# Attention's score and value products as three fp32r products of high and low parts

## The chip, the cores and the metric

The kernel runs on one core of a Trainium2 chip. The metric is the device time of one execution in microseconds. A profiled execution is read beside it; its times come from the hardware profiler.

## The reference

One block of a hybrid layer on x of 256 rows and 2048 columns, all float32. Cut to what matters here:

```python
hn = rms_norm(x, norm_w)
proj = hn @ w_in          # q, k, v, z_a, z_s, xbc, dt_raw, g_a, g_s
for window, dilation in ((128, 1), (512, 4), (2048, 16)):
    scores = q @ k.T * 128 ** -0.5 + alibi      # per head, 16 heads of 128
    o, lse = softmax(masked scores) @ v, logsumexp(masked scores)
o_a = (sum over patterns of softmax(lse) * o) * silu(z_a)
y = rms_norm(ssd_scan(silu(conv(xbc)), softplus(dt_raw), ...) * silu(z_s), ssm_norm_w)
merged = sigmoid(g_a) * (o_a @ w_attn_branch) + sigmoid(g_s) * (y @ w_ssm_branch)
out = rms_norm(x + merged @ w_out, final_norm_w)
```

With 256 rows the three attention patterns see the same scores under three masks. The kernel computes one softmax over the scores, weighted by how many patterns admit each pair (`count_c`).

## The kernel before

**Products in parts.** Nearly all weights are read once, from `wall`, in units of 128 x 1024 float32 (512 KB). `unit(n)` makes of each a high part `h` (a copy to the type fp32r, ScalarE, L271) and a low part `l` (the difference, VectorE, L272). The activations are kept in the same two parts; a product is then the sum of three fp32r products: high with high, high with low, low with high. `triple` in `gemm_pair` writes them (L471 to L473). `split` (L279, L281) makes the two parts of an activation: a copy on ScalarE, a difference on VectorE. `h` and `l` have four buffers each, `w` five.

**The stages, in order.** The scan's projections (`xs`, `zs`, `B`, `C`, with the scan between), its branch product (`ssm`), `v`, the 16 heads of attention with `q`, `k` and `za` of each head, then `ga`, `attn` and `out`. `ssm`, `v`, `ga`, `attn` and `out` go through `gemm_pair`: blocks of two times 512 columns, in which some groups of four units (`S_QUADS`) take seven products in place of eight. Their extra parts `ht` and `lt` come from the pool `mul`, two buffers each.

**A projection in attention.** `gemm_a` takes two units; each holds eight blocks of 128 x 128 weights, and each block gives one matmul of 512 columns (L324: high weights with both parts of x) and one of 256 (L327: low weights with x's high part): 32 matmuls for each of `q`, `k`, `za`. `evac` adds the two halves of the result: ScalarE copies one out of PSUM (`lo_k`, L378), VectorE adds the other (L380).

**The heads.** `qT` and `kT` are float32, 128 x 256. `scores` (L1022, L1023) multiplies them by float32 matmuls: 128 rows of queries with 128 keys, and the other 128 with all 256. The scores are then scaled, masked and made into `p` (128 x 384) by VectorE and ScalarE (`t`, `st`, `p`). `turn_p` turns the three blocks of `p` on TensorE (L1046, `ptp`) and ScalarE copies them out as `pT` (L1047). `mix` (L1053, L1054) multiplies `vt` and `pT` by float32 matmuls of 256 and of 128 columns, and gates and splits the result into `oaT`. The work is put into the stream of projections by ticks: each projection is a tick, and `after(n, f)` runs f n ticks later. So while head h+1's `q` begins, TensorE has the mix of head h-2, the turn of head h-1 and the scores of head h. A scheduler then sets each engine's order from its own estimates; each engine runs its instructions in that order, and waits where an operand is late.

**Other transfers around it.** `sum_jobs` fetches weights into `th_a` in attention, forms sums on VectorE and stores them for the later stages. `keep_left` stores left factors for the `attn` stage through `sxt_o` (pool `mul`, tag `ht`) to `sxd_o`. In the out stage four blocks of x go to `fin`, each behind a unit of weights: POOL writes one column of the block after that unit's `h` is made (L624), and then SP issues the load (L625). `fin` takes the memory of `vt`.

Of the kernel before, what the change touches and what calls it, by code (L numbers as in the profile page):

```python
# [9 lines left out]
F32 = mybir.dt.float32  # L10
F32R = mybir.dt.float32r
AF = mybir.ActivationFunctionType
# [3 lines left out]
P = 128  # L16
S = 256
# [45 lines left out]
LEFT_EVERY, ATT_EVERY = 11, 4  # L63
SUM_LAG = 3
ROOM_SSM = 2

OFF_Q, OFF_K, OFF_V, OFF_ZA = 0, D, 2 * D, 3 * D
OFF_ZS = 4 * D
# [123 lines left out]
def hybrid_block(ctx: ExitStack, tc: tile.TileContext, wall, xt, x, pk_d, cst_d, fw_d, out):  # L192
# [98 lines left out]
    def two_kts(t, q):  # L291
        t, q = (t[q // 4], q % 4) if isinstance(t, list) else (t, q)
        return t[:, 2 * q : 2 * q + 2, :]
# [4 lines left out]
    def after(ticks, f, inside=0):  # L298

        due.append((now[0] + ticks + inside / 2, f))  # L300
# [53 lines left out]
    def project(tag, acc=None):  # L354
        return gemm_a(tag, lambda kt: XT[:, kt, :], acc)
# [56 lines left out]
    def keep_left(key, x, spare, t):  # L412

        sx = t.bitcast(F32R).rearrange("p (e n s) -> p e n s", e=2, n=4)[:, :, spare:]
        turn_x(sx, t.rearrange("p (n m) -> p n m", n=2), x, spare)
        spill(lefts, key, f"sxd_{key[0]}{key[1]}", sx.bitcast(F32), [2, 4 - spare, P])
# [36 lines left out]

    seats = {}

    def gemm_pair(tag, x_of, n_kt, sxs, swap, extra={}, close=1, order=None, room={}):


# [7 lines left out]

        def banks(ts, s):
            return [bank(t, 4 if t == "g" else 2, f"{s}_{name}_{n}") for n, t in enumerate(ts)]

        def triple(acc, xh, xl, h, l, start, stop):  # L470
            pe.matmul(acc, xh, h, start=start, stop=False)  # L471
            pe.matmul(acc, xh, l, start=False, stop=False)  # L472
            pe.matmul(acc, xl, h, start=False, stop=stop)  # L473

        es = banks(e_tags, "ps")
        prods = []
# [538 lines left out]
    with tc.tile_pool(name="att", bufs=2) as ap:  # L1015
        ev = ap

        oaT = [half_kts("oaTa", "yo0a")]

        def scores(h, q, k, p):  # L1020
            sps = bank("m1", 2, f"sps{h}")
            pe.matmul(sps[:, :P], q[:, :P], k[:, :P], start=True, stop=True)  # L1022
            pe.matmul(sps[:, P:384], q[:, P:], k, start=True, stop=True)  # L1023
            t = cpool.tile([P, 384], F32, name=f"t{h}", tag="ssq")
            slope = 2.0 ** (-8.0 * (h + 1) / NH)
            ve.scalar_tensor_tensor(t, dist_c, slope / SCALE, sps[:, :384], ALU.mult, ALU.add)
            st = ap.tile([P, 8], F32, name=f"st{h}", tag="st", bufs=1)
            parts = ((0, P), (P, 384))
            for i, (a, b) in enumerate(parts):
                ve.tensor_reduce(st[:, i : i + 1], t[:, a:b], mybir.AxisListType.X, ALU.max)  # L1030
            ve.tensor_scalar(st[:, 2:4], st[:, 0:2], -SCALE, None, ALU.mult)
            for i, (a, b) in enumerate(parts):
                ac.activation(p[:, a:b], t[:, a:b], AF.Exp, scale=SCALE, bias=st[:, 2 + i : 3 + i])
            for i, (a, b) in enumerate(parts):
                ve.scalar_tensor_tensor(
                    p[:, a:b], p[:, a:b], 1.0, count_c[:, a:b], ALU.mult, ALU.mult,
                    accum_out=st[:, 4 + i : 5 + i],
                )
            ve.reciprocal(st[:, 6:8], st[:, 4:6])
            for i, (a, b) in enumerate(parts):  # L1040
                ve.tensor_scalar(p[:, a:b], p[:, a:b], st[:, 6 + i : 7 + i], None, ALU.mult)

        def turn_p(h, p, pT):
            tps = bank("m1", 2, f"ptp{h}")
            for i in range(3):
                pe.transpose(tps[:, i * P : (i + 1) * P], p[:, i * P : (i + 1) * P], ident)  # L1046
            ac.activation(pT, tps[:, :384], AF.Copy)  # L1047

        def mix(h, pT, za):
            ops = bank("m2", 2, f"ops{h}")  # L1050
            o = za
            hs = slice(h * P, (h + 1) * P)
            pe.matmul(ops[:, :S], vt[:, 0, hs], pT[:, :S], start=True, stop=False)  # L1053
            pe.matmul(ops[:, P:S], vt[:, 1, hs], pT[:, S:384], start=False, stop=True)  # L1054
            ve.tensor_tensor(o, ops[:, :S], za, ALU.mult)
            if h == 8:
                oaT.append(half_kts("oaTb", "yo0b"))
            split(o, kt_of(oaT, h)[:, :S], kt_of(oaT, h)[:, S:])
            q = h // 2
            if h % 2 == 1 and q in ATT_QUADS:  # L1060
                keep_left(("o", q), two_kts(oaT, q), 0, mul.tile([P, UNIT], F32, name=f"sxt_o{q}", tag="ht", bufs=2))

        sum_jobs(
            SUMS_ATT, range(FIRST[("q", 0)] + 7, N_UNITS, ATT_EVERY),
            [
                (th_a[:, i, :UNIT], th_a[:, 1, UNIT + 512 * i : UNIT + 512 * i + 512], th_a[:, 0, UNIT:])
                for i in range(2)
            ],
        )

        for h in range(NH):
            q, k = (ap.tile([P, S], F32, name=f"{n}T{h}", tag=f"{n}T", bufs=2) for n in "qk")

            for n, d in (("q", q), ("k", k)):
                evac(project((n, h)), d, f"{n}{h}")
            p = ap.tile([P, 384], F32, name=f"p{h}", tag="p", bufs=2)
            pT = ap.tile([P, 384], F32, name=f"pT{h}", tag="pT", bufs=1)
            za = ap.tile([P, S], F32, name=f"za{h}", tag="za", bufs=3)
            after(S_LAG + (6, 4, 2)[max(h - 13, 0)], lambda a=(h, pT, za): mix(*a))
            after(S_LAG + (3 if h < 15 else 1), lambda a=(h, p, pT): turn_p(*a))  # L1080
            after(S_LAG + (h == 0), lambda a=(h, q, k, p): scores(*a))
            zh = ev.tile([P, S], F32, name=f"zah{h}", tag="eh", bufs=2)
            evac(project(("za", h)), zh, f"za{h}", scale=0.5)
            half_silu(zh, za, f"za{h}")

        for n, q in enumerate(ATT_QUADS):
            fetch_left(
                sx_of_o, xl if n else xk, max(1, n and len(SX_X) - 1), ("o", q), two_kts(oaT, q), 0, FIRST[("ga", 2)] + O_BEHIND[n]
            )
        room = {"wt": [th_a[:, i, UNIT:] for i in range(2)]}  # L1090
        for c in (0, 2):
            es, prods = gemm_pair(
                ("ga", c), lambda kt: XT[:, kt, :], KT, sx_of_x, c == 2, order=G_ORDERS[c], room=room
            )
            open_gate(c, es, prods)
        tick(final=True)

    with tc.tile_pool(name="fin", bufs=2) as fp:
# [36 lines left out]
        for n in range(4):  # L1135
            i, cs = n // 2, slice(n % 2 * UNIT, (n % 2 + 1) * UNIT)
            behind_unit(
                FIRST[("out", 0)] + (1, 3, 5, 8)[n],
                lambda behind, i=i, cs=cs: fetch(fin[:, i, cs], x[i * P : (i + 1) * P, cs], behind),
            )  # L1140

# [79 lines left out]
```

## Time and profile before

| | us |
|---|---|
| median of 3 runs | 1387.36 (1385.95 to 1387.86) |
| the profiled execution | 1384.94 |
| its span, first to last instruction | 1383.1 |
| TensorE busy (PE) | 1373.2 |
| weight loads busy (PEld) | 1169.1 |
| VectorE busy (DVE) | 1164.5 |
| ScalarE busy (ACT) | 834.2 |
| GpSimd busy (POOL) | 138.6 |

The granted TensorE clock is 0.999 of full speed. In the rows below, a line gives the engine, the line of the kernel, the operation, the tile written and those read, the shape, and how often. A float32 matmul leaves two records, an fp32r matmul one. Matmuls overlap their ends, so the distance between the starts of two matmuls tells more than the duration of one.

### The profile page before, as it was taken

Reading aid. Unit: us, or ns where it says so; the run is one execution under the profiler, and the core shown is the slowest. Engines: PE = TensorE matmul, PEld = TensorE weight load, DVE = VectorE, ACT = ScalarE, POOL = GpSimd, SP = SyncE. Lnnn points to the kernel's source line nnn. Section 1 sums busy time; section 2 is a strip of 40 time slices with the busy share of each in tenths; the row PEclk is TensorE's granted clock in tenths of the full one; section 3 lists DMA queues with packets and bytes.
Section 4 is the critical chain, followed back from the end, with each engine's and each line's share of the span. In section 5 each row is a group of like instructions: output and inputs, shape, how many; then the busy total and the mean of one; then the engine's idle time right before and its main releaser. Section 6 shows DMA issues by size and latency. Waiting matters only on the chain.

```text
span 1383.1 us, 20652 instructions
## 1 busy us (share of the span) xinstructions
PE 1373.2 (99%) x7260; PEld 1169.1 (85%) x7260; DVE 1164.5 (84%) x1742; ACT 834.2 (60%) x1300; POOL 138.6 (10%) x222
## 2 busy tenths in 40 slices
PE   9999999999999999999999999999999999999997
PEld 8888888888888888888888888888888888888886
DVE  7898999987798898788888897777877788888997
ACT  7656677675667675766564554544544556655564
POOL 2301111101011100010000001111111000000110
PEclk9999999999999999999999999999999999999999
DMA  9657888768787866568678558888888747865763
GB/s 342 237 192 228 306 264 281 279 216 279 246 272 232 296 218 204 186 227 279 226 264 287 200 193 279 282 271 280 292 290 299 244 163 263 291 223 180 274 258 107
DMA packets 104648, 343.96 MB, mean 249 GB/s; under 512 B 11680, under 2 KB 13664, under 8 KB 104416
## 3 DMA queue, kind: packets, MB, share of 16 engines
q1 hardware_dynamic: 103824, 341.46, 72.2%
q8 instruction: 57, 0.93, 0.3%
q10 hardware_dynamic: 720, 1.18, 0.2%
q14 instruction: 47, 0.39, 0.1%
HBM read 314.34 MB, written 28.25 MB: 248 GB/s over the span
## 4 chain that ended last, share of the span: by engine, by line
PE 98%; DMA 0%; DVE 0%; POOL 0%; SPq 0%; ACT 0%; issue 0%; POOLq 0%; DVEq 0%; ACTq 0%
PE ps_zs L324 8%; PE ps_xs L324 8%; PE ps_zs L327 4%; PE ps_k L324 4%; PE ps_q L324 4%; PE ps_za L324 4%; PE ps_xs L327 4%; PE ps_ssm L471 3%; PE ps_ssm L472 3%; PE ps_ssm L473 3%; PE ps_q L327 2%; PE ps_k L327 2%; PE ps_za L327 2%; PE ps_gs L409 2%; PE ps_gs L407 2%; PE ps_gs L408 2%
## 5 line engine op out<-in xcount | busy, mean ns | idle before, releaser
L271 ACT ACTIVATE h<-w 128x1024 fp32r<-128x1024 f32 (+1 forms) x400 | 416.0, 1048 | 330.9 <-issue 79.6
L272 DVE TENSOR_TENSOR l<-w,h 128x1024 fp32r<-128x1024 f32 (+1 forms) x400 | 482.1, 1212 | 128.8 <-ACT h L271 126.5
L324 PE MATMUL ps_zs<-XT,h 128*128 128x512 f32 x496 | 176.2, 396 | 0.0
L324 PE MATMUL ps_xs<-XT,h 128*128 128x512 f32 x496 | 175.9, 396 | 0.0
L327 PE MATMUL ps_zs<-XT,l 128*128 128x256 f32 x496 | 139.7, 282 | 0.0
L327 PE MATMUL ps_xs<-XT,l 128*128 128x256 f32 x496 | 139.6, 281 | 0.0
L324 PEld LDWEIGHTS ps_xs<-XT,h 128*128 128x128 f32 x496 | 93.1, 188 | 21.8
L324 PEld LDWEIGHTS ps_zs<-XT,h 128*128 128x128 f32 x496 | 93.1, 188 | 21.4
L327 PEld LDWEIGHTS ps_zs<-XT,l 128*128 128x128 f32 x496 | 93.6, 189 | 1.5 <-issue 0.9
L327 PEld LDWEIGHTS ps_xs<-XT,l 128*128 128x128 f32 x496 | 93.6, 189 | 0.4
L324 PE MATMUL ps_q<-XT,h 128*128 128x512 f32 x256 | 92.3, 404 | 0.0
L324 PE MATMUL ps_k<-XT,h 128*128 128x512 f32 x256 | 89.8, 394 | 0.0
L324 PE MATMUL ps_za<-XT,h 128*128 128x512 f32 x256 | 89.5, 394 | 0.0
L327 PE MATMUL ps_q<-XT,l 128*128 128x256 f32 x256 | 71.0, 277 | 0.0
L327 PE MATMUL ps_k<-XT,l 128*128 128x256 f32 x256 | 71.0, 277 | 0.0
L327 PE MATMUL ps_za<-XT,l 128*128 128x256 f32 x256 | 70.9, 277 | 0.0
L529 ACT ACTIVATE ha<-wa 128x1024 fp32r<-128x1024 f32 x42 | 44.3, 1055 | 35.7 <-PE ps_ssm L473 9.1
L530 DVE TENSOR_TENSOR ltu<-wa,htu 128x1024 fp32r<-128x1024 f32 x42 | 51.3, 1223 | 12.7 <-ACT htu L529 12.5
L530 DVE TENSOR_TENSOR la<-wa,ha 128x1024 fp32r<-128x1024 f32 x42 | 51.3, 1222 | 10.8 <-ACT ha L529 10.6
L529 ACT ACTIVATE htu<-wa 128x1024 fp32r<-128x1024 f32 x42 | 44.3, 1054 | 24.2 <-PE ps_ssm L473 7.2
L324 PEld LDWEIGHTS ps_k<-XT,h 128*128 128x128 f32 x256 | 48.0, 188 | 11.2
L324 PEld LDWEIGHTS ps_za<-XT,h 128*128 128x128 f32 x256 | 48.0, 188 | 11.1
(657 smaller groups left out, 3305.1 us busy)
## 6 DMA issues: line engine op xcount, KB each, us to landing
w<-in_wall SPq DMA_DIRECT2D x396, 512.0 KB, 4.6
wa<-in_wall SPq DMA_DIRECT2D x42, 512.0 KB, 4.9
th_a<-in_wall SPq DMA_DIRECT2D x19, 512.0 KB, 5.4
sums_at<-in_wall SPq DMA_DIRECT2D x18, 512.0 KB, 4.0
acb<-acum_d SPq DMA_DIRECT2D x32, 256.0 KB, 3.7
t_ssm<-sums_at SPq DMA_DIRECT2D x13, 512.0 KB, 4.1
wt<-t_ssm SPq DMA_DIRECT2D x13, 512.0 KB, 5.1
th_a<-in_wall SPq DMA_DIRECT2D x19, 256.0 KB, 5.8
```

The costliest lines, as they stand in the source:

```text
L271: ac.activation(h[:, a:b], w[:, a:b], AF.Copy)
L272: ve.tensor_tensor(l[:, a:b], w[:, a:b], h[:, a:b].bitcast(F32), ALU.subtract)
L324: pe.matmul(acc, h[:, kk, :], m, start=(kt == 0), stop=False)
L327: pe.matmul(acc[:, S:], l[:, kk, :], m[:, :S], start=False, stop=(kt == KT - 1))
L407: pe.matmul(accs[i], xh, h[:, kk], start=(kt == 0), stop=False)
L408: pe.matmul(accs[i], xh, l[:, kk], start=False, stop=False)
L409: pe.matmul(accs[i], xl, h[:, kk], start=False, stop=(kt == KT - 1))
L471: pe.matmul(acc, xh, h, start=start, stop=False)
L472: pe.matmul(acc, xh, l, start=False, stop=False)
L473: pe.matmul(acc, xl, h, start=False, stop=stop)
L529: ac.activation(h, src, AF.Copy)
L530: ve.tensor_tensor(l, src, h.bitcast(F32), ALU.subtract)
```

## The change

Queries and keys are split into high and low parts after `evac` (tiles `qk_parts`, in the two `lt` buffers of the pool `mul`); `qT` and `kT` share one buffer. The turned `p` is split into `pT` and `pl`, and the head's columns of `vt` into `vhl`. The scores and the products with v go through `triple`, which moves out of `gemm_pair`: three fp32r matmuls for each float32 one. The last `sxt_o` takes a part of `th_a` in place of an `ht` buffer. The loads of x for the output go behind the units 1, 5, 9 and 12 of the out stage in place of 1, 3, 5 and 8.

```diff
--- before.py
+++ after.py
@@ -63,6 +63,7 @@
 LEFT_EVERY, ATT_EVERY = 11, 4
 SUM_LAG = 3
 ROOM_SSM = 2
+X_BEHIND = 1, 5, 9, 12
 
 OFF_Q, OFF_K, OFF_V, OFF_ZA = 0, D, 2 * D, 3 * D
 OFF_ZS = 4 * D
@@ -453,6 +454,11 @@
 
     seats = {}
 
+    def triple(acc, xh, xl, h, l, start, stop):
+        pe.matmul(acc, xh, h, start=start, stop=False)
+        pe.matmul(acc, xh, l, start=False, stop=False)
+        pe.matmul(acc, xl, h, start=False, stop=stop)
+
     def gemm_pair(tag, x_of, n_kt, sxs, swap, extra={}, close=1, order=None, room={}):
 
 
@@ -466,11 +472,6 @@
 
         def banks(ts, s):
             return [bank(t, 4 if t == "g" else 2, f"{s}_{name}_{n}") for n, t in enumerate(ts)]
-
-        def triple(acc, xh, xl, h, l, start, stop):
-            pe.matmul(acc, xh, h, start=start, stop=False)
-            pe.matmul(acc, xh, l, start=False, stop=False)
-            pe.matmul(acc, xl, h, start=False, stop=stop)
 
         es = banks(e_tags, "ps")
         prods = []
@@ -1017,10 +1018,15 @@
 
         oaT = [half_kts("oaTa", "yo0a")]
 
+        qkp = [
+            mul.tile([P, UNIT], F32R, name=f"qk_parts{n}", tag="lt", bufs=2).rearrange("p (n e s) -> p n e s", n=2, e=2)
+            for n in range(2)
+        ]
+
         def scores(h, q, k, p):
             sps = bank("m1", 2, f"sps{h}")
-            pe.matmul(sps[:, :P], q[:, :P], k[:, :P], start=True, stop=True)
-            pe.matmul(sps[:, P:384], q[:, P:], k, start=True, stop=True)
+            for out_ap, qs, ks in ((sps[:, :P], slice(0, P), slice(0, P)), (sps[:, P:384], slice(P, S), slice(0, S))):
+                triple(out_ap, *(t[:, qs] for t in q), *(t[:, ks] for t in k), start=True, stop=True)
             t = cpool.tile([P, 384], F32, name=f"t{h}", tag="ssq")
             slope = 2.0 ** (-8.0 * (h + 1) / NH)
             ve.scalar_tensor_tensor(t, dist_c, slope / SCALE, sps[:, :384], ALU.mult, ALU.add)
@@ -1040,25 +1046,25 @@
             for i, (a, b) in enumerate(parts):
                 ve.tensor_scalar(p[:, a:b], p[:, a:b], st[:, 6 + i : 7 + i], None, ALU.mult)
 
-        def turn_p(h, p, pT):
+        def turn_p(h, p, pT, pl, vhl):
             tps = bank("m1", 2, f"ptp{h}")
             for i in range(3):
                 pe.transpose(tps[:, i * P : (i + 1) * P], p[:, i * P : (i + 1) * P], ident)
-            ac.activation(pT, tps[:, :384], AF.Copy)
-
-        def mix(h, pT, za):
+            split(tps[:, :384], pT, pl)
+            split(vt[:, :, h * P : (h + 1) * P], vhl[:, 0], vhl[:, 1])
+
+        def mix(h, pT, pl, vhl, za):
             ops = bank("m2", 2, f"ops{h}")
             o = za
-            hs = slice(h * P, (h + 1) * P)
-            pe.matmul(ops[:, :S], vt[:, 0, hs], pT[:, :S], start=True, stop=False)
-            pe.matmul(ops[:, P:S], vt[:, 1, hs], pT[:, S:384], start=False, stop=True)
+            for b, cs, ks in ((0, slice(0, S), slice(0, S)), (1, slice(P, S), slice(S, 384))):
+                triple(ops[:, cs], vhl[:, 0, b], vhl[:, 1, b], pT[:, ks], pl[:, ks], start=(b == 0), stop=(b == 1))
             ve.tensor_tensor(o, ops[:, :S], za, ALU.mult)
             if h == 8:
                 oaT.append(half_kts("oaTb", "yo0b"))
             split(o, kt_of(oaT, h)[:, :S], kt_of(oaT, h)[:, S:])
             q = h // 2
             if h % 2 == 1 and q in ATT_QUADS:
-                keep_left(("o", q), two_kts(oaT, q), 0, mul.tile([P, UNIT], F32, name=f"sxt_o{q}", tag="ht", bufs=2))
+                keep_left(("o", q), two_kts(oaT, q), 0, mul.tile([P, UNIT], F32, name=f"sxt_o{q}", tag="ht", bufs=2) if q < ATT_QUADS[-1] else th_a[:, 1, :UNIT])
 
         sum_jobs(
             SUMS_ATT, range(FIRST[("q", 0)] + 7, N_UNITS, ATT_EVERY),
@@ -1069,15 +1075,20 @@
         )
 
         for h in range(NH):
-            q, k = (ap.tile([P, S], F32, name=f"{n}T{h}", tag=f"{n}T", bufs=2) for n in "qk")
-
-            for n, d in (("q", q), ("k", k)):
-                evac(project((n, h)), d, f"{n}{h}")
+            qk = []
+            for n, name in enumerate("qk"):
+                d = ap.tile([P, S], F32, name=f"{name}T{h}", tag="qkT", bufs=1)
+                evac(project((name, h)), d, f"{name}{h}")
+                qk.append([qkp[h % 2][:, n, e] for e in range(2)])
+                split(d, *qk[-1])
+            q, k = qk
             p = ap.tile([P, 384], F32, name=f"p{h}", tag="p", bufs=2)
-            pT = ap.tile([P, 384], F32, name=f"pT{h}", tag="pT", bufs=1)
+            pT = ap.tile([P, 384], F32R, name=f"pT{h}", tag="pT", bufs=1)
+            pl = ap.tile([P, 384], F32R, name=f"pl{h}", tag="pl", bufs=1)
+            vhl = ap.tile([P, 2, 2, P], F32R, name=f"vhl{h}", tag="vhl", bufs=1)
             za = ap.tile([P, S], F32, name=f"za{h}", tag="za", bufs=3)
-            after(S_LAG + (6, 4, 2)[max(h - 13, 0)], lambda a=(h, pT, za): mix(*a))
-            after(S_LAG + (3 if h < 15 else 1), lambda a=(h, p, pT): turn_p(*a))
+            after(S_LAG + (6, 4, 2)[max(h - 13, 0)], lambda a=(h, pT, pl, vhl, za): mix(*a))
+            after(S_LAG + (3 if h < 15 else 1), lambda a=(h, p, pT, pl, vhl): turn_p(*a))
             after(S_LAG + (h == 0), lambda a=(h, q, k, p): scores(*a))
             zh = ev.tile([P, S], F32, name=f"zah{h}", tag="eh", bufs=2)
             evac(project(("za", h)), zh, f"za{h}", scale=0.5)
@@ -1135,7 +1146,7 @@
         for n in range(4):
             i, cs = n // 2, slice(n % 2 * UNIT, (n % 2 + 1) * UNIT)
             behind_unit(
-                FIRST[("out", 0)] + (1, 3, 5, 8)[n],
+                FIRST[("out", 0)] + X_BEHIND[n],
                 lambda behind, i=i, cs=cs: fetch(fin[:, i, cs], x[i * P : (i + 1) * P, cs], behind),
             )
 
```

In the order of TensorE's instructions at the turn to the next head, before: the last matmul of `za` of one head, the mix, the turn and the scores, and the next head's `q`.

```order
L327 MATMUL ps_za_9337<-XT,l_9363 128x256
L1053 MATMUL ops_9390<-pT_8947,vt 128x256
L1054 MATMUL ops_9390<-pT_8947,vt 128x128
L1046 MATMUL ptp_9396<-cst,p_9135 128x128 x3
L1022 MATMUL sps_9401<-kT_9200,qT_9199 128x128
L1023 MATMUL sps_9401<-kT_9200,qT_9199 128x256
L324 MATMUL ps_q_9417<-XT,h_9420 128x512
L327 MATMUL ps_q_9417<-XT,l_9421 128x256
```

The same place with the change; the lines are those of the changed kernel (L458 to L460 are `triple`, L325 and L328 the projection).

```order
L328 MATMUL ps_za_9402<-XT,l_9428 128x256
L458 MATMUL ops_9454<-pT_8976,vhl_8978 128x256
L459 MATMUL ops_9454<-pl_8977,vhl_8978 128x256
L460 MATMUL ops_9454<-pT_8976,vhl_8978 128x256
L458 MATMUL ops_9454<-pT_8976,vhl_8978 128x128
L459 MATMUL ops_9454<-pl_8977,vhl_8978 128x128
L460 MATMUL ops_9454<-pT_8976,vhl_8978 128x128
L1052 MATMUL ptp_9464<-cst,p_9181 128x128 x3
L325 MATMUL ps_q_9492<-XT,h_9495 128x512
L328 MATMUL ps_q_9492<-XT,l_9496 128x256
L458 MATMUL sps_9472<-qk_parts_8483 128x128
L325 MATMUL ps_q_9492<-XT,h_9495 128x512
```

The mix has six matmuls in place of two, and of the six score products only the first stands here, two projection rows after the turn. The other five follow eight projection rows further on in this head (14 in every other head):

```order
L328 MATMUL ps_q_9492<-XT,l_9496 128x256
L459 MATMUL sps_9472<-qk_parts_8483 128x128
L460 MATMUL sps_9472<-qk_parts_8483 128x128
L458 MATMUL sps_9472<-qk_parts_8483 128x256
L459 MATMUL sps_9472<-qk_parts_8483 128x256
L460 MATMUL sps_9472<-qk_parts_8483 128x256
L325 MATMUL ps_q_9492<-XT,h_9495 128x512
```

They stand as one piece between two pairs of the same projection; before, the scores stood ahead of the whole projection.

VectorE's order at the same place before: from the weights' low part ahead of `kT` (the sum that makes k) to the steps after the scores (`t`, `st`).

```order
L272 TENSOR_TENSOR l_9448<-w_9445,h_9447 128x1024
L380 TENSOR_TENSOR kT_9200<-ps_k_9276,lo_k_9330 128x256
L272 TENSOR_TENSOR l_9478<-w_9475,h_9477 128x1024
L1055 TENSOR_TENSOR za_8948<-ops_9390,za_8948 128x256
L272 TENSOR_TENSOR l_9500<-w_9497,h_9499 128x1024
L382 SCALAR_TENSOR_TENSOR zah_9336<-ps_za_9337,lo_za_9382 128x256
L1026 SCALAR_TENSOR_TENSOR t_9404<-dc,sps_9401 128x384
L281 TENSOR_TENSOR oaTa<-za_8948,oaTa 128x256
L1030 TENSOR_REDUCE st_9406<-t_9404 128x1
L392 SCALAR_TENSOR_TENSOR za_9335<-th_za_9385,zah_9336 128x256
L1030 TENSOR_REDUCE st_9406<-t_9404 128x1
```

And with the change, over the same stretch; `qk_parts<-kT` is the low part of k, `vhl` that of v, `pl` that of p.

```order
L273 TENSOR_TENSOR l_9523<-w_9520,h_9522 128x1024
L381 TENSOR_TENSOR kT_9336<-ps_k_9337,lo_k_9391 128x256
L273 TENSOR_TENSOR l_9556<-w_9553,h_9555 128x1024
L282 TENSOR_TENSOR qk_parts_8483<-kT_9336,qk_parts_8483 128x256
L1061 TENSOR_TENSOR za_8979<-ops_9454,za_8979 128x256
L273 TENSOR_TENSOR l_9578<-w_9575,h_9577 128x1024
L383 SCALAR_TENSOR_TENSOR zah_9401<-ps_za_9402,lo_za_9447 128x256
L282 TENSOR_TENSOR vhl_9184<-vt,vhl_9184 128x256
L282 TENSOR_TENSOR pl_9183<-ptp_9464,pT_9182 128x384
L282 TENSOR_TENSOR oaTa<-za_8979,oaTa 128x256
L393 SCALAR_TENSOR_TENSOR za_9400<-th_za_9450,zah_9401 128x256
L1032 SCALAR_TENSOR_TENSOR t_9479<-dc,sps_9472 128x384
```

The low part of k stands behind one more `l`; those of v and p stand after `zah`, and the reading of the scores (`t`) has moved behind `oaTa` and `za`.

## The prediction

> **What bounds the kernel now.** I read the page first: span, busy times and the chain that ended last.
>
> ```profile
> span 1383.1 us, 20652 instructions
> PE 1373.2 (99%) x7260; PEld 1169.1 (85%) x7260; DVE 1164.5 (84%) x1742; ACT 834.2 (60%) x1300; POOL 138.6 (10%) x222
> PE 98%; DMA 0%; DVE 0%; POOL 0%; SPq 0%; ACT 0%; issue 0%; POOLq 0%; DVEq 0%; ACTq 0%
> ```
>
> TensorE carries 98% of the chain, so a matmul that takes longer or shorter moves the end by as much, and work of another engine counts only if TensorE comes to wait for it. Next the busy times by stretch: almost thirteen heads of attention, and the stretch in which x is loaded for the output. The columns are the microseconds of the stretch, then PE, PEld, DVE, ACT and POOL busy.
>
> ```profile
> 888.00:1120.00 232.00, 232.00 (x1360) 204.11 (x1359) 174.44 (x341) 114.58 (x179) 35.05 (x46) 1.00 0.79 270
> 1283.00:1300.00 17.00, 17.00 (x77) 13.94 (x77) 16.78 (x23) 6.77 (x9) 5.23 (x4) 1.00 0.71 240
> ```
>
> A busy TensorE may hide short waits, since ends are modelled; so I go by starts. The timeline of TensorE at one turn of heads (start, duration of the merged group, line, tile):
>
> ```profile
> 918.14 0.28 PE L327 MATMUL ps_za<-XT,l 128*128 128x256 f32 x1
> 918.26 0.59 PE L1053 MATMUL ops<-pT,vt 128*128 128x256 f32 x2
> 918.69 0.38 PE L1054 MATMUL ops<-pT,vt 128*128 128x128 f32 x2
> 918.91 0.49 PE L1046 MATMUL ptp<-cst,p 128*128 128x128 f32 x3
> 919.24 0.39 PE L1022 MATMUL sps<-kT,qT 128*128 128x128 f32 x2
> 919.46 0.60 PE L1023 MATMUL sps<-kT,qT 128*128 128x256 f32 x2
> 919.71 0.58 PE L324 MATMUL ps_q<-XT,h 128*128 128x512 f32 x1
> 920.12 0.28 PE L327 MATMUL ps_q<-XT,l 128*128 128x256 f32 x1
> 920.24 0.40 PE L324 MATMUL ps_q<-XT,h 128*128 128x512 f32 x1
> 920.47 0.28 PE L327 MATMUL ps_q<-XT,l 128*128 128x256 f32 x1
> ...
> 937.19 0.49 PE L1046 MATMUL ptp<-cst,p 128*128 128x128 f32 x3
> ```
>
> One float32 matmul is two passes (x2). The products with v start at 918.26 and the transposes at 918.91, so they cost 0.65. The fp32r matmul of 512 columns (L324) takes 920.47 - 920.24 = 0.23, that of 256 columns (L327) 920.24 - 920.12 = 0.12. The first L324 after the scores is recorded too early; counted back from its follower it began at 920.12 - 0.23 = 919.89, so the scores take 919.89 - 919.24 = 0.65. A head lasts 937.19 - 918.91 = 18.28. These starts leave TensorE no pause in attention: the change can win only what its own matmuls take less.
>
> **TensorE's part of the change.** Each head loses 1.30 us of float32 matmuls and gets twelve fp32r ones: for the scores three of 128 columns and three of 256, for v the same. The six of 256 have a row: 0.12 by the timeline, 0.115 if the 0.23 of 512 columns is halved; I take 0.115. Of 128 columns no fp32r matmul is in this trace, and six per head, 96 in all, make the difference. Three rows bound it from below. Every matmul loads its own weights; the pace of such loads shows where the matmuls between are only two columns wide, and the groups give their durations (last number but one: mean ns):
>
> ```profile
> 596.87 0.64 PEld L943 LDWEIGHTS tot_y<-cst,ssq 128*128 128x128 f32 x5
> 597.43 0.19 PEld L472 LDWEIGHTS ps_ssm<-l,yTa 128*128 128x128 f32 x1
> L472 PEld LDWEIGHTS ps_ga<-l,XT 128*128 128x128 f32 x64 | 12.0, 188 | 2.4
> L1022 PEld LDWEIGHTS sps<-kT,qT 128*128 128x128 f32 x32 | 4.8, 191 | 0.0
> ```
>
> Five loads in 0.64, the last of 0.19, are four steps of (0.64 - 0.19)/4 = 0.112. Those are float32 weights, but a load of fp32r weights lasts the same 188 ns as a float32 one of 191, and L327's 0.12 for 256 columns sits on this floor too. From above: a float32 matmul of 128 columns takes two passes, 919.46 - 919.24 = 0.22, and nothing here shows that a narrow fp32r matmul escapes that price.
>
> By the floor a group costs 3 x 0.112 + 3 x 0.115 = 0.68 against 0.65, that is 0.03 more; with 0.12 for each of the six it is 0.72, or 0.07 more. I take 0.04: 16 heads x 2 groups x 0.04 = 1.3 us more (0.7 to 2.2). I choose the floor because it is nearest in kind: fp32r rows of 512 and 256 columns fall with the columns (0.23 to 0.12), so the streaming of 128 would be shorter than a load, and the load is what is left. By the upper end a group costs 3 x 0.22 + 0.345 = 1.0, or 0.35 more, 32 x 0.35 = 11.2 us more.
>
> **The other engines' part.** Per head VectorE gets three differences of 256 elements (parts of q, k, v) and one of 384 read from PSUM; ScalarE three copies of 256, and its copy of the turned p stays, with another type.
>
> ```profile
> L281 DVE TENSOR_TENSOR oaTa<-za,oaTa 128x256 fp32r<-128x256 f32 x7 | 2.9, 420 | 0.0
> L1026 DVE SCALAR_TENSOR_TENSOR t<-dc,sps 128x384 f32<-128x384 f32 x12 | 6.5, 544 | 0.0
> L279 ACT ACTIVATE oaTa<-za 128x256 fp32r<-128x256 f32 x7 | 2.9, 418 | 0.0
> L271 ACT ACTIVATE h<-w 128x1024 fp32r<-128x1024 f32 x75 | 79.5, 1060 | 105.3 <-issue 35.7 <-PE ps_za L324 24.3 <-PE ps_q L324 15.1
> ```
>
> VectorE: 3 x 0.42 + 0.54 = 1.8 us a head; it idles (232 - 174.44) x 18.28/232 = 4.5 now, so 2.7 are left. ScalarE: 1.25 against 9.2 idle. Both queues stand behind TensorE in the stream of weights: ScalarE's idle time before h ends with matmuls that free its buffers, so h and l run ahead. I cost this work at nothing; uncovered it would be up to 16 x 1.8 = 29 us, reached only if no buffer ran ahead.
>
> The new wait is TensorE's, for the parts of k. Behind the waiting score products stand the projections of the next head, and behind those everything else. The chain now, in the same head (ScalarE, then VectorE):
>
> ```profile
> 913.89 0.36 ACT L378 ACTIVATE lo_k<-ps_k 128x256 f32<-128x256 f32 x1
> 915.57 1.06 ACT L271 ACTIVATE h<-w 128x1024 fp32r<-128x1024 f32 x1 [1.31 <-PE ps_za L324]
> 915.16 0.42 DVE L380 TENSOR_TENSOR kT<-ps_k,lo_k 128x256 f32<-128x256 f32 x1
> 916.66 1.23 DVE L272 TENSOR_TENSOR l<-w,h 128x1024 fp32r<-128x1024 f32 x1 [1.08 <-ACT h L271]
> ```
>
> kT is there at 915.58. The order puts the high part behind one h: 916.63 + 0.42 = 917.05; and the low part behind one l: 917.89 + 0.42 = 918.3. The scores stood at 919.24 and their low products now stand 10 projection rows later (16 in other heads), that is five pairs of 0.35 or 1.75 us. The slack is 0.9 + 1.75 = 2.7 us, so no wait. p's parts and v's parts are made right after the turn and used a head later, 18 us on.
>
> Two tiles move: q's and k's parts sit in the two `lt` buffers, which the ga stage wants back after the last scores, and the last `sxt_o` goes to th_a. SP's queue keeps its spill (`sxd_o`) between the same weight loads; the loads of `fin` for attn_2 and attn_4 come earlier there, since vt is read out sooner. POOL's order does not change. Nothing here has a price I can read; I give it nothing, and put waits in the ga stage under a rival.
>
> **The x loads.** The third and fourth go from behind units 5 and 8 of the out stage to behind 9 and 12, with their POOL copies.
>
> ```profile
> L624 POOL COPY fin<-h x4: 463/570/3624, 1283.4 to 1299.1; 128x1 f32<-128x1 f32 x4
> L625 SPq DMA_DIRECT2D fin<-in_x x4: 328/328/423, 1287.0 to 1299.7; - x4
> L1162 DVE TENSOR_TENSOR fin<-fin,spare x4: 1218/1220/1220, 1331.9 to 1367.9; 128x1024 f32<-128x1024 f32 x4
> DMA to landing us min/median/max: 2.3/3.5/8.3
> ```
>
> The loads issue up to 1299.7 and are first read at 1331.9. Unit 12 comes about seven units after unit 5, 12 matmuls of 0.23 or 2.8 us each: 1299.7 + 20 + 8.3 = 1328 at the latest, and the fourth is read only with the second pair of blocks. They delay nothing; nor can they help, for TensorE does not pause at 1283 to 1300 (17.00 of 17.00 busy). Priced at nothing; uncovered it is one landing, 3.5 to 8.3 us.
>
> **Sum.** The profiled execution took 1384.94 us, 1.84 more than its span. It becomes 1384.94 + 1.3 = 1386.2. The median of the runs, 1387.36, is 2.4 above that execution; I add the difference to the median: 1388.7.
>
> **Rivals.** The bound for "same" is 0.2%, 2.8 us, about what a measurement of this kernel can tell from no change.
>
> (1) Slower: narrow fp32r matmuls run at float32's pace, 0.22 each in place of 0.112. For it speaks that every fp32r row of the trace has 256 columns or more, and that the only rows of 128 columns are float32; against it the fall from 512 to 256. Time 1387.36 + 11.2 = 1398.6. It decides from (2.8 - 1.3)/96 = 0.016 above the floor, that is from about 0.128 per narrow matmul.
>
> (2) Faster: the loads of fp32r weights are not the limit. Streaming halves with the columns, so 128 would take 0.06, a group 3 x 0.06 + 0.345 = 0.525, 0.125 less than now: 32 x 0.125 = 4.0 us less, 1383.4. Against it: the 188 ns of those loads and the 0.12 of L327. The Trainium skill, "TensorE: Matmul & The Clock Gate", section Back-to-back issue gap, has a measured sustained pace of about 81 ns for 128 columns with loads between; by it a group costs about 0.59 and the whole change wins about 2 us, an estimate from that page. The trace does not show it: its smallest step between full loads is 0.112, so I hold it unlikely for 4-byte weights.
>
> (3) Slower: TensorE waits. If k's low part came 3 us later than I reckon, 0.3 us a head, 15 heads 4.5 us more; or as much once in the ga stage for the returned `lt` buffers: 1388.7 + 4.5 = 1393.2. For it speaks that the order itself sets the scores back by 10 to 16 rows; against it the slack of 2.7.
>
> **How the numbers follow.** Floor case 0.42, of which 0.04 ends over 0.2% with small waits; rival 1 0.34, rival 3 0.14, rival 2 0.08 (0.02 of it within 0.2%), the rest, 0.02, unnamed waits. Same 0.38 + 0.02 = 0.40; slower 0.04 + 0.34 + 0.14 + 0.02 = 0.54; faster 0.06. The point is the floor case's, the likeliest single one, 1388.7, by itself 1388.1 to 1389.6. The range leaves out rival 2 and the tail of rivals 1 and 3: from 1386.0, a win of 1.4, to 1400.5, rival 1 with 0.24 per narrow matmul.
>
> **What would show it.** In the new profile: the step between starts of the score products of 128 columns, 0.11 (right) or 0.22 (rival 1) or 0.06 (rival 2); a head of about 18.36 against 18.28 from transposes to transposes; no row of TensorE with an idle time before it ended by `qk_parts`, `pl` or `vhl`; VectorE near 85% in attention. I am wrong if the heads lengthen by more than 0.2 us, or if the heads fit and the time beyond attention moves by more than 1 us.

## The result and the profile after

The changed kernel takes 1398.03 us (median of 6 runs, 1396.34 to 1399.72); the kernel before takes 1386.40 beside it (6 runs, 1385.39 to 1387.86). The ratio is 1.0085, with a 95% interval of 1.0075 to 1.0095: 11.6 us slower. First the page of the changed kernel: span, busy times, and the chain that ended last.

```profile
span 1396.5 us, 20897 instructions
PE 1379.7 (99%) x7324; PEld 1173.6 (84%) x7324; DVE 1186.8 (85%) x1806; ACT 848.5 (61%) x1348; POOL 144.2 (10%) x222
PE 93%; DMA 3%; DVE 2%; ACT 1%; issue 1%; POOL 0%; SPq 0%; POOLq 0%; DVEq 0%; ACTq 0%
```

The span grew by 13.4 us, TensorE's busy time by 6.5 only, and the chain now contains DMA, VectorE and ScalarE: somewhere TensorE waits. By the starts of the stages, 7.35 us of the 13.4 lie in the out stage (first to last `ps_out`: 98.30 in place of 90.95), 2.7 in fourteen heads of attention, and the rest in small pieces, of which 1.0 comes before the scan, where nothing was changed.

**Attention.** The timeline of TensorE at one turn of heads: the six products with v, the transposes, and a little later the score products.

```profile
921.14 0.28 PE L458 MATMUL ops<-pT,vhl 128*128 128x256 f32 x1
...
921.50 0.22 PE L458 MATMUL ops<-pT,vhl 128*128 128x128 f32 x1
921.56 0.28 PE L459 MATMUL ops<-pl,vhl 128*128 128x128 f32 x1
921.67 0.28 PE L460 MATMUL ops<-pT,vhl 128*128 128x128 f32 x1
921.78 0.51 PE L1052 MATMUL ptp<-cst,p 128*128 128x128 f32 x3
...
923.99 0.22 PE L459 MATMUL sps<-qk_parts 128*128 128x128 f32 x1
924.05 0.27 PE L460 MATMUL sps<-qk_parts 128*128 128x128 f32 x1
924.16 0.33 PE L458 MATMUL sps<-qk_parts 128*128 128x256 f32 x1
```

The products of 128 columns step by 0.11 (921.56 to 921.67 to 921.78, and 924.05 to 924.16 in the scores); only the first behind a 256 steps by 0.06 (from 921.50, and from 923.99). The mix takes 921.78 - 921.14 = 0.64, as the float32 mix did (0.65). By the same kind of starts the six score products take 0.69 in place of 0.65, and the turn 0.36 in place of 0.33. No row of TensorE in the heads waits for `qk_parts`, `pl` or `vhl`. VectorE is 191.37/232 = 82% busy in the same stretch as before:

```profile
888.00:1120.00 232.00, 232.00 (x1392) 205.31 (x1392) 191.37 (x393) 126.78 (x217) 31.17 (x46) 1.00 0.81 271
```

**The out stage.** TensorE's timeline at the first group of seven products (columns as above, and in brackets the wait ahead and what ended it), and the stretch at the lower clock (busy TensorE, weight loads, VectorE, ScalarE, POOL, then the granted clock):

```profile
1324.10 0.79 PE L458 MATMUL pp_out<-htt,mT 128*128 128x512 f32 x1 [4.46 <-ACT htt L530]
...
1328.91 0.60 PE L458 MATMUL ps_out<-htu,mT 128*128 128x512 f32 x1
1329.34 0.41 PE L459 MATMUL ps_out<-lc,sx_m 128*128 128x512 f32 x1
1322.54:1329.36 6.82, 5.24 (x12) 3.62 (x13) 6.37 (x9) 6.37 (x9) 0.83 (x2) 0.50 0.58 184
```

TensorE's last matmul ahead of the group ends at 1319.64; then it stands still for 4.46 us. At 1322.54, within the wait, the granted clock falls to 0.50, and it stays there until 1329.36: steps of 0.43 (1328.91 to 1329.34) in place of 0.23. The 11 matmuls from 1324.10 to 1329.34 took 5.24 where 2.5 were needed, 2.7 lost: some 2.2 by the clock, the rest in longer steps ahead of weights that ScalarE made late. Wait and clock together are 7.2 of the 7.35 us. What TensorE waited for, read backwards: ScalarE, then SP's queue, then POOL:

```profile
1322.99 1.06 ACT L530 ACTIVATE htt<-room_o 128x1024 fp32r<-128x1024 f32 x1 [9.06 <-DMA room_o<-t_out]
1314.26 0.43 SPq L517 DMA_DIRECT2D room_o<-t_out  x1
1311.06 0.33 SPq L626 DMA_DIRECT2D fin<-in_x  x1
SPq L626 <- POOL fin L625: 14.1, 2, 8.8
1301.62 9.54 POOL L625 COPY fin<-h 128x1 f32<-128x1 f32 x2 [8.34 <-ACT h L272]
L625 POOL COPY fin<-h x4: 178/2242/9419, 1289.4 to 1325.8; 128x1 f32<-128x1 f32 x4
```

`htt` is made of `room_o`, whose load was issued at 1314.26 and took 8.7 us to land. It stood in SP's queue behind the second x load, and that load stood until 1311.06 for POOL's copy of one column. The row of 1301.62 merges two copies; the first is the longest of the last row, 9.42 us (that row gives the shortest, median and longest of the four, in ns). VectorE at that time:

```profile
1301.62 0.69 DVE L1125 SCALAR_TENSOR_TENSOR th_a<-th_a,fin 128x512 f32<-128x512 f32 x1
1302.21 2.36 DVE L273 TENSOR_TENSOR l<-w,h 128x1024 fp32r<-128x1024 f32 x2
...
1309.77 1.23 DVE L531 TENSOR_TENSOR la<-wa,ha 128x1024 fp32r<-128x1024 f32 x1
1312.49 1.89 DVE L282 TENSOR_TENSOR mT<-mtp,mT 128x512 fp32r<-128x512 f32 x3 [1.50 <-ACT mT L280]
```

VectorE runs from 1301.62 to 1311.00 without a pause, all of it on instructions that read two tiles; the copy ends at 1311.04. So the theory to test is: GpSimd's copy cannot run beside such a run, SP stands behind the copy, and the loads for the seven products stand behind SP.

### The profile page after: what moved, and what is told of

Its sections match the earlier page's. It is cut to its first block, busy times and chain, and to the rows that moved or that the text cites. A ratio compares the mean times of both kernels' runs of the same rounds, so it can differ in the third digit from the quotient of the medians.

```text
span 1396.5 us, 20897 instructions
## 1 busy us (share of the span) xinstructions
PE 1379.7 (99%) x7324; PEld 1173.6 (84%) x7324; DVE 1186.8 (85%) x1806; ACT 848.5 (61%) x1348; POOL 144.2 (10%) x222
## 4 chain that ended last, share of the span: by engine, by line
PE 93%; DMA 3%; DVE 2%; ACT 1%; issue 1%; POOL 0%; SPq 0%; POOLq 0%; DVEq 0%; ACTq 0%
PE ps_zs L325 8%; PE ps_xs L325 8%; PE ps_q L325 4%; PE ps_zs L328 4%; PE ps_k L325 4%; PE ps_za L325 4%; PE ps_xs L328 4%; PE ps_ssm L458 3%; PE ps_ssm L459 3%; PE ps_ssm L460 3%; PE ps_za L328 2%; PE ps_q L328 2%; PE ps_k L328 2%; PE ps_gs L409 2%; PE ps_gs L408 2%; PE ps_gs L410 2%
## 5 line engine op out<-in xcount | busy, mean ns | idle before, releaser
L325 PE MATMUL ps_zs<-XT,h 128*128 128x512 f32 x496 | 176.2, 396 | 0.0
L325 PE MATMUL ps_xs<-XT,h 128*128 128x512 f32 x496 | 175.9, 396 | 0.0
L328 PE MATMUL ps_zs<-XT,l 128*128 128x256 f32 x496 | 139.7, 282 | 0.0
L328 PE MATMUL ps_xs<-XT,l 128*128 128x256 f32 x496 | 139.6, 281 | 0.0
L325 PEld LDWEIGHTS ps_xs<-XT,h 128*128 128x128 f32 x496 | 93.1, 188 | 21.8
L325 PEld LDWEIGHTS ps_zs<-XT,h 128*128 128x128 f32 x496 | 93.1, 188 | 21.4
L328 PEld LDWEIGHTS ps_zs<-XT,l 128*128 128x128 f32 x496 | 93.6, 189 | 1.5 <-issue 0.9
L325 PE MATMUL ps_q<-XT,h 128*128 128x512 f32 x256 | 93.8, 403 | 0.5 <-ACT h L272 0.5
L328 PEld LDWEIGHTS ps_xs<-XT,l 128*128 128x128 f32 x496 | 93.6, 189 | 0.4
L325 PE MATMUL ps_k<-XT,h 128*128 128x512 f32 x256 | 90.3, 395 | 0.0
L325 PE MATMUL ps_za<-XT,h 128*128 128x512 f32 x256 | 90.3, 395 | 0.0
L328 PE MATMUL ps_q<-XT,l 128*128 128x256 f32 x256 | 71.7, 280 | 0.0
L328 PE MATMUL ps_za<-XT,l 128*128 128x256 f32 x256 | 71.7, 280 | 0.0
L328 PE MATMUL ps_k<-XT,l 128*128 128x256 f32 x256 | 71.7, 280 | 0.0
L325 PEld LDWEIGHTS ps_za<-XT,h 128*128 128x128 f32 x256 | 48.0, 188 | 11.3
L325 PEld LDWEIGHTS ps_k<-XT,h 128*128 128x128 f32 x256 | 48.0, 188 | 11.3
L325 PEld LDWEIGHTS ps_q<-XT,h 128*128 128x128 f32 x256 | 48.1, 188 | 10.4 <-ACT h L272 0.9
```

The lines of the kernel that those rows point to most:

```text
L325: pe.matmul(acc, h[:, kk, :], m, start=(kt == 0), stop=False)
L328: pe.matmul(acc[:, S:], l[:, kk, :], m[:, :S], start=False, stop=(kt == KT - 1))
```

## The experiments

Medians are of this kernel and of the kernel before on the same chip; ratios are to the kernel before.

| run | us | before | ratio, 95% interval |
|---|---|---|---|
| e1_x_back | 1391.78 | 1386.61 | 1.0050 (1.0031 to 1.0069) |
| e2_x_alone | 1391.33 | 1386.61 | 1.0035 (1.0023 to 1.0047) |
| e3_act_marks | 1389.96 | 1386.61 | 1.0026 (1.0016 to 1.0035) |
| e4_mix_only | 1391.49 | 1386.61 | 1.0033 (1.0020 to 1.0046) |
| e5_scores_only | 1391.64 | 1386.17 | 1.0035 (1.0025 to 1.0045) |
| e6_scores_whole | 1389.69 | 1386.17 | 1.0025 (1.0012 to 1.0038) |
| e7_before_rows | 1387.71 | 1386.17 | 1.0013 (1.0001 to 1.0025) |
| e8_after_rows | 1387.43 | 1386.17 | 1.0005 (0.9995 to 1.0014) |
| e9_scan_rows | 1384.10 | 1386.12 | 0.9986 (0.9977 to 0.9995) |
| e10_vec_pause | 1393.43 | 1386.12 | 1.0050 (1.0038 to 1.0063) |
| e11_x_alone_act | 1385.56 | 1386.12 | 0.9996 (0.9987 to 1.0005) |

**Is it the x loads?** Undo their move, and do it alone.

```diff
-X_BEHIND = 1, 5, 9, 12
+X_BEHIND = 1, 3, 5, 8     # e1, in the changed kernel
-                FIRST[("out", 0)] + (1, 3, 5, 8)[n],
+                FIRST[("out", 0)] + (1, 5, 9, 12)[n],     # e2, in the kernel before
```

> The changed kernel with its x loads back behind units 1, 3, 5 and 8 of the out stage; attention stays as changed. Theory (the 7.4 us that the out stage grew by come from the spread of the x loads, the other 5 or so from attention, ga and v): 1398.0 - 7.2 = about 1390.8, and the 4.46 us wait of TensorE at the first seven-product group of out is gone. Rival A (the narrow fp32r products carry the loss, and the wait in out is their late echo): no change, 1397 to 1398.

> The kernel before with only the x loads moved behind units 1, 5, 9 and 12; attention stays float32. Theory: the same queue is blocked here, so 1386.4 plus up to 7.4, about 1393; less if VectorE's run of work at that place leaves GpSimd's copies a pause. Rival A: 1386.4, the loads are harmless by themselves.

Undoing it gains about 6 us, 1391.8 (five of its seven runs took 1390.2 to 1391.9, two, of which there is no profile, 1398.5 and 1400.0), and in the profiled execution the long wait is gone (0.39 is left at another place). Alone it costs about 5 in a kernel whose attention is untouched. In that run (e2) the second copy, the first of the two merged below, takes 8.17 us and ends at 1305.11, 0.04 after VectorE's instruction of 1303.85; TensorE then waits 2.97, and from 1319.66 to 1323.07 it has half the clock (last row; columns as above):

```profile
1296.94 8.29 POOL L624 COPY fin<-h 128x1 f32<-128x1 f32 x2 [8.57 <-DMA w<-in_wall]
1303.85 1.22 DVE L272 TENSOR_TENSOR l<-w,h 128x1024 fp32r<-128x1024 f32 x1
1317.97 0.50 PE L471 MATMUL pp_out<-htt,mT 128*128 128x512 f32 x1 [2.97 <-ACT htt L529]
1319.67:1323.07 3.40, 3.40 (x8) 2.26 (x8) 3.40 (x6) 2.87 (x4) 1.47 (x2) 0.50 0.35 89
```

Rival A falls: a good part of the loss is made by moving three of the four x loads, in a kernel whose attention products are untouched.

**Is it the later transfer, or the copy ahead of it?** Keep the loads where the change puts them, and let ScalarE write the one column.

```diff
-fetch(fin[:, i, cs], x[...], behind)          # gp.tensor_copy, then nc.sync.dma_start
+ac.activation(fin[:, i, cs.start : cs.start + 1], behind, AF.Copy)
+nc.sync.dma_start(fin[:, i, cs], x[...])
```

> The changed kernel, x loads behind units 1, 5, 9 and 12 as changed; only the one-column copy ahead of each x load is made by ScalarE in place of GpSimd, so that it cannot be kept waiting by VectorE. TensorE's and VectorE's order is the same. Theory (the second copy took 9.42 us on GpSimd while VectorE ran without a pause, SP stood behind it, and the loads for the seven-product group behind that): x loads issue 8 us earlier, the wait of 4.46 us and the half clock after it go, 1390.8. Rival B (the later x loads harm by sharing the transfers with the weights): the wait stays, 1396 to 1398.

> The kernel before with the x loads moved behind units 1, 5, 9 and 12 and their marks made by ScalarE. Theory (the spread costs only through GpSimd's copy): no wait of TensorE, 1386.2, against 1391.3 with GpSimd's marks. Rival B (the later loads harm by themselves): about 1391.

Both came out as the theory said: 1389.96 in the changed kernel (e3), 1385.56 in the kernel before (e11; not to be told from no change). In e3, SP's queue issues the second x load and the first `room_o` at

```profile
1300.87 0.33 SPq L1150 DMA_DIRECT2D fin<-in_x  x1
1308.38 0.33 SPq L517 DMA_DIRECT2D room_o<-t_out  x1
```

10.2 and 5.9 us earlier than in the changed kernel, or 8.7 and 4.4 when the 1.5 is taken off by which this run's out stage began earlier; and TensorE has no wait in the out stage. TensorE's and VectorE's instructions stand in the same order in e3 as in the changed kernel, and the transfers are the same, so rival B falls: the later loads are harmless. ScalarE's copies took 0.18 to 0.21 us each in e3. The copy on GpSimd in front of the loads cost 1398.03 - 1389.96 = 8.1 us, or 8.3 with each kernel taken against the kernel before beside it.

**Is it VectorE that holds the copy?** Put one instruction with a single input into VectorE's run, and leave the rest of the changed kernel as it is.

```diff
+if n == FIRST[("out", 0)] + 5:     # in unit(), ahead of the low parts' users
+    with tc.high_priority(L_AHEAD):
+        ve.tensor_reduce(pause[0], h[:, :256].bitcast(F32), mybir.AxisListType.X, ALU.max)
```

> The changed kernel as it is, GpSimd's marks and the x loads behind units 1, 5, 9 and 12, with one more instruction: VectorE reduces 256 columns of the sixth unit's high part to one column, right ahead of that unit's low part, so that one instruction with a single input from SBUF stands in VectorE's run. Theory (GpSimd's copy reads SBUF and gets no turn while VectorE runs instructions with two inputs from SBUF): the copy of 9.42 us takes about 2, the second x load goes out near 1304, the wait at the seven-product group is gone, 1390.5. Rival H (the copy waits for something else, such as fin being free of its readers): the copy ends near 1311 again, 1398.

POOL, VectorE and TensorE in that run, and the stretch behind TensorE's wait:

```profile
1299.87 1.85 POOL L630 COPY fin<-h 128x1 f32<-128x1 f32 x1 [8.34 <-ACT h L274]
1301.61 0.41 DVE L278 TENSOR_REDUCE pause<-h 128x1 f32<-128x256 f32 x1
1304.99 4.61 POOL L630 COPY fin<-h 128x1 f32<-128x1 f32 x1 [3.27 <-ACT h L274]
1308.35 1.21 DVE L536 TENSOR_TENSOR la<-wa,ha 128x1024 fp32r<-128x1024 f32 x1
1318.98 0.50 PE L463 MATMUL pp_out<-htt,mT 128*128 128x512 f32 x1 [1.10 <-ACT htt L535]
1319.00:1326.00 7.00, 6.55 (x27) 5.01 (x28) 7.00 (x12) 6.33 (x9) 0.83 (x2) 1.00 0.65 200
```

The copy of 9.42 us takes 1.85, and ends (1301.73) while the added reduction runs. The third copy, which asks behind it, finds no such instruction; it takes 4.61 and ends at 1309.60, where VectorE's run ends (1308.35 + 1.21 = 1309.56). That keeps a wait of 1.10 us in place of 4.46, after which the granted clock is 1.00. The mechanism is as the theory says, rival H falls (readers of `fin` start as late as 1303.07, after the copy's end); the size is not: 1393.4 in place of 1390.5. The copy that followed was caught in the rest of the same run, and the out stage is 2.7 us longer than in e3 (93.56 against 90.89). In all profiles the copies ahead of x loads that took more than 0.4 us end 0.04 to 0.05 us behind the end of an instruction of VectorE: they get in at the boundary of two instructions, here at the one ahead of the reduction.

The Trainium skill, "SBUF — State Buffer", section Who interferes with whom, has this rule: a VectorE instruction with two inputs in SBUF contends with a GpSimd instruction that reads SBUF, for ports that the two share under an exclusive lock. The trace agrees with it: 9.42 and 4.61 us to the end of a run, 8.17 through most of one, and 1.85 with one single-input instruction in the run. The rule does not give the length of it: that the copy can lose at ten boundaries of a run, one after another, is what these rows add.

**Attention.** What is left, 3.4 us in e3, is made there for the most part: in e3's profile the stretch from the first `ps_q` to the first `ps_ga` is 2.8 us longer than before, with the last head's scores (0.7) moved out of it, and the stretch from there to the first `ps_out` 1.4 longer, with those scores in it. The length of a head, from transposes to transposes (with 921.78 above), and sixteen pairs of projections (512 then 256 columns) of two heads, by their first start and that of the next projection:

```profile
884.78 0.30 PE L1052 MATMUL ptp<-cst,p 128*128 128x128 f32 x1
891.47 0.40 PE L325 MATMUL ps_k<-XT,h 128*128 128x512 f32 x1
897.12 0.40 PE L325 MATMUL ps_za<-XT,h 128*128 128x512 f32 x1
903.42 0.30 PE L1052 MATMUL ptp<-cst,p 128*128 128x128 f32 x1
910.05 0.39 PE L325 MATMUL ps_k<-XT,h 128*128 128x512 f32 x1
915.60 0.39 PE L325 MATMUL ps_za<-XT,h 128*128 128x512 f32 x1
```

One head takes 903.42 - 884.78 = 18.64, the next 921.78 - 903.42 = 18.36. In the first a pair takes (897.12 - 891.47)/16 = 353 ns, in the second (915.60 - 910.05)/16 = 347. Before, every head took 18.28, and the pairs 347. Eight of the fourteen whole heads are like the second (0.07 more than before), six like the first (0.35 more). The first theory was that the scores, broken into two pieces, cost 0.12 a head and shift the pace. Three runs, of which the third has ScalarE's marks:

```diff
-triple(...) for the scores                       # e4: float32 scores, q and k not split, only the mix in parts; x loads as e1
+pe.matmul(sps[...], q[...], k[...])
-triple(...) for the mix                          # e5: float32 mix, only the scores in parts; x loads as e1
+pe.matmul(ops[...], vt[...], pT[...])
-after(S_LAG + (h == 0), ... scores)              # e6: scores behind the whole next q, in one piece
+after(S_LAG + (h < 15), ... scores)
```

> As the changed kernel with the x loads back behind units 1, 3, 5, 8, and with only the products with v as three fp32r products; the scores are float32 matmuls on float32 q and k again, and stand as one piece ahead of the next q. Theory (the six products with v cost what the two float32 ones did, 0.64 us; the scores in two pieces cost 0.12 us a head more and shift the projections to their slower pace of 353 ns a pair, 1.6 us in all): 1390.8 - 1.9 - 1.6 = 1387.3, with every pair of projections in attention at 346.6 ns. Rival C (the slower pace comes from the extra work of VectorE and ScalarE or from any fp32r narrow product): the pace stays mixed, about 1389 to 1390.8.

> As the changed kernel with the x loads back behind units 1, 3, 5, 8, and with only the scores as three fp32r products; the products with v are float32 matmuls again. Theory (the products with v are neutral, the scores cost 0.12 us a head more because their six products stand in two pieces): products in attention 1.9 us above the kernel before as with both, 1390 to 1392 by the pace that the projections fall into. Rival D (the products with v carry the 1.9): products as before, about 1389.

> The changed kernel with ScalarE's marks for the x loads, and the scores one projection later, behind the whole q of the next head, so that their six products stand in one piece. Theory (the break in the piece costs 0.12 us a head): products in attention 1.9 us less than with ScalarE's marks alone, 1390.0 - 1.9 = 1388.1 at the same pace of the projections, 1386.5 if all projections fall into 346.6 ns a pair, 1390.8 if all fall into 353.2. Rival E (the products cost what they cost, in one piece or two): 1390.0.

The theory fell. In e4 the scores are the float32 pair again and stand ahead of the whole q, as before, and yet nearly all heads take the slow pace:

```profile
921.33 0.30 PE L1052 MATMUL ptp<-cst,p 128*128 128x128 f32 x1
939.94 0.30 PE L1052 MATMUL ptp<-cst,p 128*128 128x128 f32 x1
```

18.61 a head. By the starts of all pairs that stand between other projection rows, the mean pair takes 346.9 ns before, 350.2 in the changed kernel, e1, e3, e5 and e10, 352.4 in e4, 349.3 in e6. A kernel's pattern of fast and slow heads was the same in each run that kept TensorE's order in attention. Over those pairs (about 690 to 730 of 768, by kernel) the slow ones cost 2.3 us more than before in the changed kernel, 4.1 in e4, 1.7 in e6. The rest of the heads' time, products and turns, is 1.2 us above before with the change, 1.0 in e5, 0.6 in e4, and 1.3 in e6: one piece or two makes no difference (rival E); by their starts the six score products take 0.69 us in one piece in e6, and 0.11 + 0.58 in two in the changed kernel. That e4 loses as much as both parts together (1391.5, against 1391.8 in e1) is the pace, not the products. e5 (1391.6) has the pace of e1, but its out stage is 1.8 us longer than e1's (93.43 against 91.59). There the fourth copy on GpSimd, behind unit 8 as in the kernel before, stood in a run of VectorE, and TensorE waited for `htt`:

```profile
1303.07 5.74 POOL L625 COPY fin<-h 128x1 f32<-128x1 f32 x1 [3.77 <-issue]
1318.38 0.50 PE L458 MATMUL pp_out<-htt,mT 128*128 128x512 f32 x1 [1.25 <-ACT htt L530]
```

So e5 came out within the 1390 to 1392 of its theory in part by luck, and with the loads back at their old units the copy can still be caught.

**Two paces: can they be avoided?** Each unit's eight products of 512 columns first, then its eight of 256.

```diff
-for kk: pe.matmul(acc, h...); pe.matmul(acc[:, S:], l...)
+for kk: pe.matmul(acc, h...)
+for kk: pe.matmul(acc[:, S:], l...)      # e7: before; e8: e3; e9: before, only in the scan's projections
```

> The kernel before with each unit's eight products of 512 columns first and its eight of 256 columns after them, in place of alternating; nothing else. About 770 pairs of the kernel before run at 353 ns and the rest at 346.6. Theory (two paces are a matter of the alternation of 512 and 256): rows of 512 run at 227 as in the out stage and rows of 256 at 113 to 120, so a pair takes 340 to 347 everywhere; 770 x 0.0064 = 4.9 us less at 347, 1381.7. Rival F (the paces come from the supply of weights or of their low parts): no change, or slower.

> The changed kernel with ScalarE's marks for the x loads and the same regrouping of the projections, eight of 512 then eight of 256. Theory: about 984 pairs lose 6.4 ns, 6.3 us less than 1390.0, 1383.7; the scores are broken into pieces still and cost their 0.12 us a head. Rival F: 1390 or slower.

> The kernel before with the regrouping (eight products of 512, then eight of 256) only in the scan's projections; attention keeps the alternation, where the kernel before runs at 346.6 ns a pair. From the run with rows everywhere: v began 1.66 us earlier than before. Theory: that 1.7 us stays, 1386.2 - 1.7 = 1384.5. Rival G (attention's pace depends on what stood before it, so that its projections fall into 353.2 and give it back): 1386 to 1389.

TensorE in e7, one unit of k and the start of the next:

```profile
906.40 2.00 PE L323 MATMUL ps_k<-XT,h 128*128 128x512 f32 x8
908.24 1.11 PE L328 MATMUL ps_k<-XT,l 128*128 128x256 f32 x8
909.19 0.63 PE L323 MATMUL ps_k<-XT,h 128*128 128x512 f32 x2
```

Eight of 512 take 1.84 and eight of 256 take 0.95, 2.79/8 = 349 ns a pair in every unit. One pace, as the theory said, but not the better one: e7 wins 1.7 us in the scan and gives 1.7 back in attention, where before all heads ran at 347; another 1.7 goes between the first `ps_ga` and the first `ps_out`, 1.1 of it in two waits for `htu` and `ltu` (1387.7, expected 1381.7). The changed kernel with ScalarE's marks loses nothing in attention by it and ends at 1387.4, 2.5 us under e3 and not to be told from the kernel before (expected 1383.7). The version that follows from this, rows in the scan and alternation in attention, beats both kernels: e9, 1384.10, 0.9986 (0.9977 to 0.9995). From the first `ps_xs` to the first `ps_v`, before and then in e9:

```profile
76.58 0.39 PE L324 MATMUL ps_xs<-XT,h 128*128 128x512 f32 x1
748.33 0.39 PE L471 MATMUL ps_v<-h,XT 128*128 128x512 f32 x1
```

```profile
77.62 0.39 PE L325 MATMUL ps_xs<-XT,h 128*128 128x512 f32 x1
747.63 0.39 PE L476 MATMUL ps_v<-h,XT 128*128 128x512 f32 x1
```

671.75 and 670.01, 1.74 us less, as expected; rival G did not come.

## Why the prediction was right in part and wrong in its sum

**The products: right, their sum in part by luck.** The floor of 0.112 us for an fp32r product of 128 columns held (0.11). The scores' group costs 0.04 more, as foreseen. The group for v costs 0.01 less, not 0.04 more, and the turn, which has no term in the sum, 0.03 more. So products and turns together came to 1.2 us where 1.3 was foreseen, and a head at the better pace takes 18.34 to 18.37 where 18.36 was foreseen. Rival 1 (0.22) and rival 2 (0.06 throughout) fell: 0.06 is seen only where a narrow product follows one of 256 columns, 0.11 between narrow ones. The Trainium skill, "TensorE: Matmul & The Clock Gate", section Back-to-back issue gap, has about 81 ns for 128 columns in a stream of loads and products. The trace does not agree: 0.11 us between narrow ones. Rival 3's wait for k's parts did not come, nor one of its size in the ga stage.

**The cover of VectorE and ScalarE: right in attention.** 82% busy against the "near 85%" foreseen, and no wait of TensorE.

**The x loads: the step that failed.** The text says of them "They delay nothing", and "uncovered it is one landing". They were priced by when x is read, 1331.9. The text speaks of the third and fourth load alone; the second moved too, from behind unit 3 to behind unit 5, and its copy is the one that took 9.42 us. What stands behind a moved load on SP's queue was not counted, though SP issues in order: here it was the first `room_o`, which TensorE needs at 1319.6. And the copies ahead of the loads got no price of their own: the row quoted for them, 463/570/3624, had in its 3624 a copy that lost at one boundary after another of a run of VectorE, and the stretch beside it had VectorE busy for 16.78 of 17.00 us. The step, priced at nothing, measured 8.1 us (e3 against the changed kernel); alone, in the kernel before, 4.7 with GpSimd's copy (e2) and nothing with ScalarE's (e11).

**The pace of the projections: not in the sum.** The pairs that the change does not touch were taken to keep the 347 ns of attention's rows; the same pair takes 353 in much of the scan. 2.3 us, and 6 of 14 heads lengthened by more than the 0.2 us that the text itself had set as its limit. Why a head falls into one pace or the other stays open.

The sum began at 1387.36, the median of three runs; over six the kernel before takes 1386.40. So the point, 1388.7, was the floor case, and the runs ended at 1398.0, near rival 1's 1398.6, by another mechanism: 1.2 us of products and turns, 2.3 of pace, 7.2 of wait and slower clock in the out stage. That 1398.0 lies inside the range, 1386.0 to 1400.5, is luck: its upper part stood there for rival 1, which did not come. By the sign that the text had set for itself, time beyond attention that moves by more than 1 us, its account was wrong: the out stage alone moved by 7.35. With the copy out of the way (e3) the change costs 3.4 us, of which 1.3 were foreseen.

## What to carry to other kernels

A transfer that is moved is not priced by when its data is read but by what its queue does behind it, and by the slowest engine that it waits for: look for the next load on the same queue that TensorE needs, and for the largest, not the median, duration of the marker in front of the moved one. A one-column copy on an idle GpSimd is not free beside a VectorE without pauses; ScalarE can write it. And where TensorE's stream is reordered, compare the pace of rows that were not touched too.

## What the hardware showed that was not expected

- A one-column copy on GpSimd took 0.18 us beside a pausing VectorE and 9.42 beside one that ran two-input instructions without a pause. That it always loses in such a run is not so: in the kernel before the copy behind the same unit took 0.61 us, inside a similar run, and in e1 0.72, though it began with the same instruction of VectorE (`th_a`, an `l` behind it) as the one of 9.42. What let those in at the first boundary is not shown.
- With a wait of 4.46 us the granted clock was 0.50 for 6.8 us (1322.54 to 1329.36, 5.2 of it with TensorE at work); after one of 1.10 it stayed at 1.00. After one of 2.97 TensorE went on at full clock for 1.7 us, with pauses between its matmuls, and then had 0.50 for 3.4 us (1319.66 to 1323.07). The Trainium skill, "TensorE: Matmul & The Clock Gate", section What's actually happening, puts the slower clock behind at least one idle window of some 3.4 us. The two slow stretches are one and two such windows long; but a pause of 2.97, shorter than a window, with a slow restart behind it, was enough here. So by these rows a pause below 3 us is not safe.
- A stream of fp32r products that alternates between 512 and 256 columns has two stable paces, 347 and 353 ns a pair, and keeps the one it fell into until other products come between; in rows of eight it has one, 349. Which pace follows which order is reproducible but not explained by these runs.
